# A two-layer decoder trunk on one core: MoBA's queries projected earlier, attention ends behind the softmax, compressed values a step later, x transposed in fewer goes

## The chip, the core and the metric

The kernel runs on one core of a Trainium2 chip. Five engines run at once, each with its own queue of instructions that it takes in order: TensorE (PE in the profile, its weight loads PEld), VectorE (DVE), ScalarE (ACT), GpSimd (POOL) and SyncE (SP), which issues most DMAs. They wait for each other by semaphores. The metric is the time of one execution on the device, in microseconds (us); lower is better.

## The reference

Two layers, 256 positions, width 1024, all in float32. Each layer is

```
x += 1/2 * SwiGLU(RMSNorm(x))                    # FFN 1: 1024 -> 2816 -> 1024
z  = RMSNorm(x) @ W_in                           # one projection, 4888 columns, split:
                                                 # q_a g kc vc ks vs kw vw | q_b k_b v_b | gate_a gate_b
A  = NSA(...)                                    # 8 heads: compressed + selected + sliding window, per-head gates
B  = MoBA(q_b, k_b, v_b)                         # 8 heads; with 256 positions one causal block
x += W_out(sigmoid(gate_a) * (A @ P_A) + sigmoid(gate_b) * (B @ P_B))
x += 1/2 * SwiGLU(RMSNorm(x))                    # FFN 2
```

and a last RMSNorm. The compressed branch takes windows of 32 keys or values at a stride of 16, sends each through a small MLP (2048 -> 128 -> 64, with a GELU between) and attends to the 15 results. Queries and keys of both attentions are turned by rotary positions (rope).

## The kernel before, in words

**Matrices.** Rows are tiled by 128 (two tiles, t = 0 and 1), weights arrive in float32 units of 1 MB and are split into a high and a low part: ScalarE makes `hi` (`split_hi`), VectorE subtracts to make `lo` (`split_lo`). Each product is three matmuls of 512 columns (`mm3`: high x high, low x high, high x low), and each `mm3` is one *tick* of a clock that the program counts while it is written out. Every third tick one half unit of a later weight is split, so `hi` and `lo` instructions stand all through ScalarE's and VectorE's queues.

**The order** of the instructions is written out by hand, with two devices. `defer(n, f)` writes `f`'s instructions n ticks later. A side generator, `attention`, is advanced a step every few ticks between the projections' matmuls (`side_step`): it does the compression, the transposes of keys and queries, and the attention itself, while `project` keeps TensorE busy. `ORDER` lists the projections (each 16 ticks, tile 0 and then tile 1, and after each tile a callback that reads the bank); the place `None` is `hidden`, the first matrix of the compression's MLP. A step of the generator waits for flags such as "KB" (the keys are projected).

**Banks.** PSUM has four tags of two banks each, used in turn: "a0" and "a1" for the large products, "tr" for transposes, "sc" for scores and the small products of the MLP. A tag's next tile waits until everything that reads its last but one tile is done.

**Names.** `kcd`, `ksd`: compressed and selected/window keys; `X2`: the flattened windows; `pK`: transposes of keys, from which ScalarE and VectorE make the high and low `ksT`; `pQ`: transposes of queries, copied to `qT` on ScalarE; `hh`: product of the MLP's first matrix, copied to `HH`; `hp`: two small transposing products of it; `hx`, `hy`, `hth`: the GELU; `hk`, `hv`: its results for keys and values; `cp`: product with the MLP's second matrix (once for keys, once for values); `kc`, `kp`, `kbd`: the compressed keys, roped, transposed, split; `vbd`: the compressed values, spread over the heads. The GELU chain runs in `compress_more`, with `yield` between its steps.

**The callbacks.** `cb_rope` (for q_a, q_b and k_b) makes, per tile, three products and a sum on VectorE (`rt`), for queries a copy to the high part on ScalarE and a subtraction to the low part on VectorE; the gates' callback is one tanh on ScalarE (`gt`).

**The attention loop.** `attend_all` takes the jobs in pairs. In iteration i it writes the values' products of pair i-2 (`s3`: matmuls `o`, and after a group's last job the end `finish`, which on VectorE divides by the sums and applies the gates, `cf` and `aS`), then the transposes of pair i-1 (`s2_`: `pt`) and the scores of pair i (`s1`: `s`), and then the softmax of pair i (`soft`: on VectorE a mask and a maximum for each job, `s` and `m`; on ScalarE the exponentials `P`).

**x transposed.** After the last product of an FFN or of `w_out`, `residual` adds it to x for tile t and column half h and defers four transposes of that quarter of x (`nrm.trans`: one "tr" bank, a product with the gains `xg` on VectorE, a high part on ScalarE and a low part on VectorE, both `hT`).

Of the kernel before, what the change touches and what calls it, by code (L numbers as in the profile page):

```python
# [9 lines left out]
F32 = mybir.dt.float32  # L10
# [7 lines left out]
HD, NH, G = 64, 8, 2  # L18
# [12 lines left out]
C_Q, C_G, C_KV2, C_QB, C_KB, C_VB, C_GA = 0, 512, 920, 1304, 1816, 2328, 2840  # L31
WIDTH = {C_G: 408, C_KV2: 384}

ORDER = [C_Q, C_KV2, C_G, C_GA, None, C_GA + 512, C_QB, C_KB, C_VB, C_GA + 1024, C_GA + 1536]

EVERY = 3
SIDE = 3
# [44 lines left out]
def hybrid_kernel(ctx: ExitStack, tc: tile.TileContext, T, out):  # L82
    nc = tc.nc
# [28 lines left out]
    def bank(tag, name, shape):  # L112

        return psum.tile(shape, F32, name=name, tag=tag)
# [104 lines left out]
    parts, ends = [], []  # L219
# [204 lines left out]
    def ffn(l, n, nrm):  # L424
# [80 lines left out]
        for t in range(NT):  # L505
            for h in range(2):
                if nxt.g is None and t == h == 1:

                    for i in range(2):
                        p = bank("tr", "dq", [128, 256])  # L510
                        for f in range(NF - TAIL, NF):
                            some(f, t, h, p, i)
                        finish(nxt, gfin, ys[t], t, h, p, i)
                    continue
                for f in range(NF - TAIL, NF):
                    some(f, t, h)
                if nxt.g is None:
                    finish(nxt, gfin, ys[t], t, h, ps[t][h])
                else:
                    residual(nxt, t, h, ps[t][h], 4 + t)  # L520
        drop(*tiles)
        return nxt

# [17 lines left out]
    def mixer(l, nrm):  # L541
# [72 lines left out]
        def scaled(name, o, coef):  # L614
            a = s2(name, [128, NH, HD])
            nc.vector.tensor_mul(a, o, coef[:, :, None].to_broadcast([128, NH, HD]))
            return a
# [46 lines left out]
        def compress_more():  # L664
            hx, th = [], []
            for j in range(2):
                hp = bank("sc", "hp", [128, G, 16])
                nc.tensor.matmul(hp.rearrange("p g c -> p (g c)"), HH[:, j], K["sel"][:, j], start=True, stop=True)
                hp = hp[:, :, 0:NC_]

                hx.append(sm.tile([128, G, NC_], F32, name="hx", bufs=2))
                nc.scalar.copy(hx[j], hp)
                y = sm.tile([128, G, NC_], F32, name="hy", bufs=1)
                nc.vector.tensor_mul(y, hx[j], hx[j])
                nc.vector.tensor_scalar(y, y, 0.044715, 1.0, op0=OP.mult, op1=OP.add)
                nc.vector.tensor_mul(y, y, hx[j])
                th.append(sm.tile([128, G, NC_], F32, name="hth", bufs=2))
                nc.scalar.activation(th[j], y, AF.Tanh, scale=float(np.sqrt(2 / np.pi)))
                nc.vector.tensor_scalar(th[j], th[j], 0.5, 0.5, op0=OP.mult, op1=OP.add)
                if j == 0:  # L680
                    nc.vector.tensor_mul(hk.rearrange("p (g c) -> p g c", g=G)[:, :, 0:NC_], th[0], hx[0])
                else:
                    for g in range(G):
                        nc.vector.tensor_mul(hv[:, 4 * g:4 * g + 4, 0:NC_],
                                             th[1][:, g, None, :].to_broadcast([128, 4, NC_]),
                                             hx[1][:, g, None, :].to_broadcast([128, 4, NC_]))
                yield None
            cp = bank("sc", "cp", [64, HD])
            nc.tensor.matmul(cp, hk, w2[0], start=True, stop=True)
            t1 = sm.tile([64, HD], F32, name="ct1", bufs=1)  # L690
            nc.vector.tensor_mul(t1, cp, K["ropec"][:, 0:HD])
            t2 = sm.tile([64, HD], F32, name="ct2", bufs=1)
            for a, b in ((0, 32), (32, 0)):
                nc.vector.tensor_mul(t2[:, a:a + 32], cp[:, b:b + 32], K["ropec"][:, HD + a:HD + a + 32])
            kc2 = sm.tile([64, 2, HD], F32, name="kc2", bufs=1)
            nc.vector.tensor_add(kc2, t1[:, None, :].to_broadcast([64, 2, HD]), t2[:, None, :].to_broadcast([64, 2, HD]))
            cp = bank("sc", "cp", [128, HD])
            nc.tensor.matmul(cp, hv.rearrange("p h c -> p (h c)"), w2[1], start=True, stop=True)
            vbd[0] = p2.tile([128, NH, HD], F32, name="vbd", tag="vbd", bufs=1)
            nc.vector.tensor_mul(vbd[0], cp[:, None, :].to_broadcast([128, NH, HD]),  # L700
                                 K["hmask"][:, :, None].to_broadcast([128, NH, HD]))
            yield None
            kp = bank("tr", "kp", [128, G, 32])
            nc.tensor.transpose(kp.rearrange("p g c -> p (g c)"), kc2.rearrange("p u d -> p (u d)"), ident[:64, :64])
            nc.scalar.copy(kbd[:, :, 0], kp[:, :, 0:16])
            nc.vector.tensor_sub(kbd[:, :, 1], kp[:, :, 0:16], kbd[:, :, 0].bitcast(F32))

        HH = sm.tile([128, 2, CMP_HIDDEN], F32, name="HH", bufs=1)

# [15 lines left out]
        def attend_all(jobs, behind):  # L725

            pairs = [jobs[i:i + 2] for i in range(0, len(jobs), 2)] + [[]] * 2
            for i in range(len(pairs)):
                for j in pairs[i - 2]:
                    j[3]()  # L730

                for a in range(2):
                    for k, d in ((2, 1), (0, 0)):
                        for j in pairs[i - d][a:a + 1]:
                            j[k]()
                for j in pairs[i]:
                    j[1]()
                side["every"] = PAIR + 1 if i == 0 else PAIR if i < len(pairs) - 1 else behind
                yield None
            side["every"] = SIDE  # L740

        def compressed(t, qT, dst):
# [28 lines left out]
            def s3():  # L771
                o = bank("a1", "co", [128, NH, HD])
                nc.tensor.matmul(o, st["pT"], vbd[0], start=True, stop=True)
                nc.gpsimd.tensor_add(dst, dst, scaled("aC", o, st["c"]))

            return s1, soft, s2_, s3

        def attend(t, heads, nj, qT, kT, v, finish):
# [6 lines left out]
            for i0 in range(0, len(items), per):  # L785
# [33 lines left out]
                def s3(i0=i0, some=some, st=st):  # L819
                    if i0 == 0:  # L820
                        O["o"] = bank("a1", "o", [128, NH, HD])
                    for i, (h, j) in enumerate(some):
                        for c in range(nk):
                            nc.tensor.matmul(O["o"][:, i0 + i], st["pT"][:, i * nk + c], v(h, c, j),  # L824
                                             start=c == 0, stop=c == nk - 1)
                    if i0 + per == len(items):
                        finish(O["o"], O["su"])

                yield s1, soft, s2_, s3

# [127 lines left out]
        nxt = Norm(3 * l + 2)  # L958
        for h in range(2):
            project((l, "w_out", h), lambda k, t: (mT[t][0][:, k], mT[t][1][:, k]), KD, 512,  # L960
                    lambda t, ps: residual(nxt, t, h, ps, 4 + t if h else 17))
        drop(*sA, *sB, *gts[0], *gts[1])
        return nxt

# [79 lines left out]
```

## Time and profile before

| | |
|---|---|
| median of 3 runs | 1176.99 us (1176.88 to 1177.00) |
| the profiled execution's own time | 1177.28 us |
| its span, first to last instruction | 1175.2 us |
| mean granted TensorE clock over the span | 0.998 of full speed |
| PE busy | 1161.5 us (99%) |
| DVE busy | 730.2 us (62%) |
| ACT busy | 586.9 us (50%) |
| DMA, mean over the span | 173 GB/s, no queue over 53% of the 16 engines |

Busy is the time with an instruction running. TensorE's instructions overlap, and the ends of its matmuls are modelled, so the distance from one start to the next tells more of its pace than the sum of their lengths. The timeline used below lists one engine's instructions in order of time: start, length, the line of the kernel, what is written from what, the shape, how many in a row, and in brackets the idle time ahead of it with what ended it. The two layers run the same program, 578.7 us apart in the mixer.

### The profile page before, as it was taken

How to read it: one execution, taken by the hardware profiler on the slowest of the kernel's cores; microseconds unless marked ns; L12 is line 12 of the kernel's file. 1: busy time of each engine (PE TensorE's matmuls, PEld its weight loads, DVE VectorE, ACT ScalarE, POOL GpSimd, SP SyncE). 2: the span in 40 equal slices, each digit the busy share in tenths (PEclk: the TensorE clock that was granted, in tenths of full speed). 3: DMA queues.
4: the chain of work that ended last, by engine and by line, in shares of the span. 5: the costliest groups of instructions: out<-in, count | busy, mean ns of one | idle time of the engine just before them, and what ended most of it. 6: DMA issues, size and time to landing. Idle time of an engine off the chain costs nothing.

```text
span 1175.2 us, 14436 instructions
## 1 busy us (share of the span) xinstructions
PE 1161.5 (99%) x5689; PEld 974.8 (83%) x5689; DVE 730.2 (62%) x1003; ACT 586.9 (50%) x929; POOL 31.2 (3%) x46
## 2 busy tenths in 40 slices
PE   8999999999999999999999999999999999999997
PEld 6888888988888888888888888889888888888886
DVE  6645546878857665545475455478787577645543
ACT  6444443567465464445364444346665644545332
POOL 2000000000100000000000000000001000000000
PEclk9999999999999999999999999999999999999999
DMA  8755462862444465555546555538434364665540
GB/s 278 258 194 179 144 243 93 208 193 94 143 143 145 143 236 193 185 174 214 180 154 204 187 188 199 174 117 217 144 109 144 117 204 125 238 208 164 180 179 36
DMA packets 103347, 203.53 MB, mean 173 GB/s; under 512 B 4560, under 2 KB 25504, under 8 KB 103280
## 3 DMA queue, kind: packets, MB, share of 16 engines
q1 hardware_dynamic: 102544, 201.84, 52.6%
q8 instruction: 45, 0.74, 0.3%
q10 hardware_dynamic: 432, 0.46, 0.1%
q0 software_dynamic: 304, 0.32, 0.1%
q14 instruction: 22, 0.18, 0.0%
HBM read 201.55 MB, written 1.05 MB: 172 GB/s over the span
## 4 chain that ended last, share of the span: by engine, by line
PE 90%; DVE 5%; ACT 3%; issue 1%; DMA 1%; SPq 0%; POOL 0%; POOLq 0%; DVEq 0%; ACTq 0%
PE pr L147 7%; PE pr L149 7%; PE pr L148 7%; PE dn L149 7%; PE dn L147 7%; PE dn L148 7%; PE u L147 6%; PE u L148 6%; PE u L149 6%; PE g L148 6%; PE g L147 6%; PE g L149 6%; PE pT L383 2%; DVE lo L237 2%; PE o L824 2%; PE gu L147 1%
## 5 line engine op out<-in xcount | busy, mean ns | idle before, releaser
L237 DVE TENSOR_TENSOR lo<-raw,hi 128x1024 fp32r<-128x1024 f32 (+3 forms) x386 | 457.0, 1214 | 209.0 <-ACT hi L230 208.7
L230 ACT CAST hi<-raw 128x1024 fp32r<-128x1024 f32 (+3 forms) x386 | 386.0, 1040 | 269.2 <-PE u L149 106.7
L147 PE MATMUL pr<-hi,hT 128*128 128x512 f32 (+2 forms) x320 | 126.0, 394 | 0.0
L147 PE MATMUL dn<-hi,aTh 128*128 128x512 f32 x318 | 124.6, 392 | 0.0
L147 PE MATMUL u<-hi,hT 128*128 128x512 f32 x320 | 124.6, 389 | 0.0
L149 PE MATMUL u<-hi,hT 128*128 128x512 f32 x320 | 124.5, 389 | 0.0
L148 PE MATMUL u<-lo,hT 128*128 128x512 f32 x320 | 124.5, 389 | 0.0
L149 PE MATMUL dn<-hi,aTl 128*128 128x512 f32 x318 | 123.8, 389 | 0.0
L148 PE MATMUL dn<-lo,aTh 128*128 128x512 f32 x318 | 123.7, 389 | 0.0
L147 PE MATMUL g<-hi,hT 128*128 128x512 f32 x312 | 123.6, 396 | 0.0
L148 PE MATMUL g<-lo,hT 128*128 128x512 f32 x312 | 121.7, 390 | 0.6 <-DVE lo L237 0.5
L149 PE MATMUL pr<-hi,hT 128*128 128x512 f32 (+2 forms) x320 | 122.0, 381 | 0.0
L148 PE MATMUL pr<-lo,hT 128*128 128x512 f32 (+2 forms) x320 | 121.7, 380 | 0.0
L149 PE MATMUL g<-hi,hT 128*128 128x512 f32 x312 | 121.7, 390 | 0.0
L385 DVE TENSOR_TENSOR aTl<-pT,aTh 128x512 fp32r<-128x512 f32 x40 | 25.8, 686 | 72.5 <-ACT aTh L384 72.5
L149 PEld LDWEIGHTS u<-hi,hT 128*128 128x128 f32 x320 | 60.1, 188 | 12.5
L147 PEld LDWEIGHTS u<-hi,hT 128*128 128x128 f32 x320 | 60.1, 188 | 12.5
L148 PEld LDWEIGHTS u<-lo,hT 128*128 128x128 f32 x320 | 60.1, 188 | 12.4
L149 PEld LDWEIGHTS dn<-hi,aTl 128*128 128x128 f32 x318 | 59.7, 188 | 12.4
L148 PEld LDWEIGHTS dn<-lo,aTh 128*128 128x128 f32 x318 | 59.7, 188 | 12.2
L147 PEld LDWEIGHTS dn<-hi,aTh 128*128 128x128 f32 x318 | 59.7, 188 | 12.0
L148 PEld LDWEIGHTS g<-lo,hT 128*128 128x128 f32 x312 | 58.7, 188 | 12.7 <-DVE lo L237 1.4
(221 smaller groups left out, 1584.8 us busy)
## 6 DMA issues: line engine op xcount, KB each, us to landing
raw<-in_ffn_wd SPq DMA_DIRECT2D x44, 1024.0 KB, 5.0
raw<-in_ffn_wu SPq DMA_DIRECT2D x40, 1024.0 KB, 5.1
raw<-in_ffn_wg SPq DMA_DIRECT2D x38, 1024.0 KB, 5.1
raw<-in_w_in SPq DMA_DIRECT2D x32, 1024.0 KB, 5.1
raw<-in_w_out SPq DMA_DIRECT2D x8, 1024.0 KB, 5.0
raw<-in_ffn_wg SPq DMA_DIRECT2D x10, 512.0 KB, 4.0
raw<-in_ffn_wu SPq DMA_DIRECT2D x8, 512.0 KB, 5.0
raw<-in_w_branch_nsa SPq DMA_DIRECT2D x4, 1024.0 KB, 5.1
```

The source lines that it names most:

```text
L147: nc.tensor.matmul(ps, x[0], w[0], start=start, stop=False)
L148: nc.tensor.matmul(ps, x[0], w[1], start=False, stop=False)
L149: nc.tensor.matmul(ps, x[1], w[0], start=False, stop=stop)
L230: nc.scalar.copy(done[i][0][:, a], raws[i][:, a])
L237: nc.vector.tensor_sub(lo[:, a], raws[i][:, a], hi[:, a].bitcast(F32))
L383: nc.tensor.transpose(p[:, k], src[:, 128 * k:128 * k + 128], ident)
L385: defer(1, lambda: nc.vector.tensor_sub(lo, p, hi.bitcast(F32)))
L824: nc.tensor.matmul(O["o"][:, i0 + i], st["pT"][:, i * nk + c], v(h, c, j), start=c == 0, stop=c == nk - 1)
```

## The change

Four edits. In `ORDER`, the projection of MoBA's queries (`C_QB`) moves to the place ahead of `None`, where the first half of the first gate (`C_GA`) stood; that half moves behind `None`, and the second half into the place that the queries left. In `attend_all`, the end of a group of heads is written after the softmax of the iteration rather than ahead of it. In `compress_more`, the values' `cp` and `vbd` move a step later, behind the keys' transpose `kp`. In `residual`'s waits, the second half of tile 0 is transposed in the tick of the first half of tile 1 (FFN), and the first half of tile 0 in the tick of its second (`w_out`). No arithmetic changes.

```diff
-ORDER = [C_Q, C_KV2, C_G, C_GA, None, C_GA + 512, C_QB, C_KB, C_VB, C_GA + 1024, C_GA + 1536]
+ORDER = [C_Q, C_KV2, C_G, C_QB, None, C_GA, C_GA + 512, C_KB, C_VB, C_GA + 1024, C_GA + 1536]
...
-                    residual(nxt, t, h, ps[t][h], 4 + t)
+                    residual(nxt, t, h, ps[t][h], 8 if h > t else 4 + t * h)
...
             nc.vector.tensor_add(kc2, t1[:, None, :].to_broadcast([64, 2, HD]), t2[:, None, :].to_broadcast([64, 2, HD]))
+            yield None
+            kp = bank("tr", "kp", [128, G, 32])
+            nc.tensor.transpose(kp.rearrange("p g c -> p (g c)"), kc2.rearrange("p u d -> p (u d)"), ident[:64, :64])
+            nc.scalar.copy(kbd[:, :, 0], kp[:, :, 0:16])
+            nc.vector.tensor_sub(kbd[:, :, 1], kp[:, :, 0:16], kbd[:, :, 0].bitcast(F32))
             cp = bank("sc", "cp", [128, HD])
             nc.tensor.matmul(cp, hv.rearrange("p h c -> p (h c)"), w2[1], start=True, stop=True)
             vbd[0] = p2.tile([128, NH, HD], F32, name="vbd", tag="vbd", bufs=1)
             nc.vector.tensor_mul(vbd[0], cp[:, None, :].to_broadcast([128, NH, HD]),
                                  K["hmask"][:, :, None].to_broadcast([128, NH, HD]))
-            yield None
-            kp = bank("tr", "kp", [128, G, 32])
-            nc.tensor.transpose(kp.rearrange("p g c -> p (g c)"), kc2.rearrange("p u d -> p (u d)"), ident[:64, :64])
-            nc.scalar.copy(kbd[:, :, 0], kp[:, :, 0:16])
-            nc.vector.tensor_sub(kbd[:, :, 1], kp[:, :, 0:16], kbd[:, :, 0].bitcast(F32))
...
-                for j in pairs[i - 2]:
-                    j[3]()
+                ends = [j[3]() for j in pairs[i - 2]]
...
                 for j in pairs[i]:
                     j[1]()
+                for end in ends:
+                    if end is not None:
+                        end()
...
-                nc.gpsimd.tensor_add(dst, dst, scaled("aC", o, st["c"]))
+                return lambda: nc.gpsimd.tensor_add(dst, dst, scaled("aC", o, st["c"]))
...
-                    if i0 + per == len(items):
-                        finish(O["o"], O["su"])
+                    return (lambda: finish(O["o"], O["su"])) if i0 + per == len(items) else None
...
-                    lambda t, ps: residual(nxt, t, h, ps, 4 + t if h else 17))
+                    lambda t, ps: residual(nxt, t, h, ps, 4 + t if h else 20 - 3 * t))
```

How instructions stand in the queues, at three places of layer 0.

ScalarE, from the projection ahead of `hidden` (its callbacks are `gt` or `qb`) to the copy of `hh`; before:

```order
L230 CAST hi<-raw 128x1024
L920 ACTIVATE gt<-pr,rh 128x512
L230 CAST hi<-raw 128x1024
L601 CAST ksT<-pK_1876 128x512
L601 CAST ksT<-pK_1882 128x512
L588 CAST qT<-pQ 128x512 x2
L920 ACTIVATE gt<-pr,rh 128x512
L230 CAST hi<-raw 128x1024
L588 CAST qT<-pQ 128x512 x2
L230 CAST hi<-raw 128x1024 x2
L721 COPY HH<-hh 128x256
```

And now:

```order
L230 CAST hi<-raw 128x1024
L535 CAST qb<-rt_1864 128x8x64
L230 CAST hi<-raw 128x1024
L601 CAST ksT<-pK_1883 128x512
L601 CAST ksT<-pK_1889 128x512
L588 CAST qT<-pQ 128x512 x2
L535 CAST qb<-rt_1931 128x8x64
L230 CAST hi<-raw 128x1024
L588 CAST qT<-pQ 128x512 x2
L230 CAST hi<-raw 128x1024 x2
L721 COPY HH<-hh 128x256
```

The two tanh, which read TensorE's bank, have become two copies, which read VectorE's sums `rt`; all else stands where it stood.

VectorE in the same stretch; before:

```order
L658 TENSOR_TENSOR X_1501<-x_1839,X_1501 128x8x2x15
L237 TENSOR_TENSOR lo<-raw,hi 128x1024 x2
L602 TENSOR_TENSOR ksT<-pK_1876,ksT 128x512
L602 TENSOR_TENSOR ksT<-pK_1882,ksT 128x512
L237 TENSOR_TENSOR lo<-raw,hi 128x1024 x5
L674 TENSOR_TENSOR hy<-hx 128x30
```

And now (the rope of tile 0, and the first row of that of tile 1):

```order
L237 TENSOR_TENSOR lo<-raw,hi 128x1024
L528 SCALAR_TENSOR_TENSOR rt_1864<-pr,r,ropeq 128x512
L532 SCALAR_TENSOR_TENSOR rt_1866<-pr,r,ropeq 128x8x32 x2
L534 TENSOR_TENSOR rt_1864<-rt_1864,rt_1866 128x512
L536 TENSOR_TENSOR qb<-rt_1864,qb 128x8x64
L237 TENSOR_TENSOR lo<-raw,hi 128x1024
L602 TENSOR_TENSOR ksT<-pK_1883,ksT 128x512
L602 TENSOR_TENSOR ksT<-pK_1889,ksT 128x512
L237 TENSOR_TENSOR lo<-raw,hi 128x1024
L528 SCALAR_TENSOR_TENSOR rt_1931<-pr,r,ropeq 128x512
```

One rope with its two waiting ends stands ahead of the `ksT` subtractions, the other behind them and one `lo`; both have left the attention loop.

VectorE from the compressed keys to the first scores; before:

```order
L691 TENSOR_TENSOR ct_2042<-cp,c_ropec 64x64
L694 TENSOR_TENSOR ct_2044<-cp,c_ropec 64x32 x2
L696 TENSOR_TENSOR kc_2047<-ct_2042,ct_2044 64x128
L700 TENSOR_TENSOR vbd<-cp,c_hmask 128x512
L237 TENSOR_TENSOR lo<-raw,hi 128x1024
L706 TENSOR_TENSOR kbd<-kp,kbd 128x2x16
L802 TENSOR_TENSOR s<-s,c_causal 128x512
```

And now:

```order
L691 TENSOR_TENSOR ct_2058<-cp,c_ropec 64x64
L694 TENSOR_TENSOR ct_2060<-cp,c_ropec 64x32 x2
L696 TENSOR_TENSOR kc_2063<-ct_2058,ct_2060 64x128
L237 TENSOR_TENSOR lo<-raw,hi 128x1024
L701 TENSOR_TENSOR kbd<-kp,kbd 128x2x16
L705 TENSOR_TENSOR vbd<-cp,c_hmask 128x512
L804 TENSOR_TENSOR s<-s,c_causal 128x512
```

`vbd` has gone behind one `lo` and `kbd`. On TensorE the values' `cp` stands between `kp` and the eight `s`, where it stood right behind the keys' `cp`.

## Rows read from the trace of the kernel before

**Rows 1.** Page: TensorE's busy time, share of the span, instructions.
```profile
PE 1161.5 (99%) x5689; PEld 974.8 (83%) x5689; DVE 730.2 (62%) x1003; ACT 586.9 (50%) x929; POOL 31.2 (3%) x46
```

**Rows 2.** TensorE's waits in all: total us, times, longest us.
```profile
PE pt L815 <- ACT P L807: 1.3, 2, 0.7
PE cp L698 <- issue: 1.2, 2, 0.6
```

**Rows 3.** Timeline of TensorE, compressed keys to attention: start, length, what.
```profile
250.60 0.33 PE L689 MATMUL cp<-w,hk 128*64 128x64 f32 x2
251.55 0.41 PE L698 MATMUL cp<-w,hv 128*128 128x64 f32 x2 [0.62 <-issue]
...
254.01 0.27 PE L704 MATMUL kp<-c_ident,kc 64*128 64x64 f32 x1
254.21 1.22 PE L796 MATMUL s<-ksT,qT 128*128 128x256 f32 x8
255.27 0.40 PE L147 MATMUL pr<-hi,hT 128*128 128x512 f32 x1
```

**Rows 4.** Timeline of VectorE in the same stretch.
```profile
252.94 0.28 DVE L696 TENSOR_TENSOR kc<-ct,ct 64x128 f32<-64x128 f32 x1
253.15 0.68 DVE L700 TENSOR_TENSOR vbd<-cp,c_hmask 128x512 f32<-128x512 f32 x1
253.75 1.21 DVE L237 TENSOR_TENSOR lo<-raw,hi 128x1024 fp32r<-128x1024 f32 x1
254.89 0.18 DVE L706 TENSOR_TENSOR kbd<-kp,kbd 128x32 fp32r<-128x32 f32 x1
254.99 0.70 DVE L802 TENSOR_TENSOR s<-s,c_causal 128x512 f32<-128x512 f32 x1
```

**Rows 5.** Timeline of TensorE, two steps of the attention loop.
```profile
271.56 1.89 PE L824 MATMUL o<-vv,pT 128*128 128x64 f32 x16
...
275.09 0.39 PE L147 MATMUL pr<-hi,hT 128*128 128x512 f32 x1
...
278.52 1.89 PE L824 MATMUL o<-vv,pT 128*128 128x64 f32 x16
...
283.35 0.39 PE L147 MATMUL pr<-hi,hT 128*128 128x512 f32 x1
```

**Rows 6.** Timeline of VectorE between those steps: rope of MoBA's queries, tile 0.
```profile
273.21 0.74 DVE L528 SCALAR_TENSOR_TENSOR rt<-pr,r,ropeq 128x512 f32<-128x512 f32 x1
...
276.16 0.69 DVE L536 TENSOR_TENSOR qb<-rt,qb 128x512 fp32r<-128x512 f32 x1 [0.69 <-ACT qb L535]
```

**Rows 7.** Timeline of ScalarE around `hidden`.
```profile
234.86 0.68 ACT L920 ACTIVATE gt<-pr,rh 128x512 f32<-128x512 f32 x1
...
236.38 1.08 ACT L601 CAST ksT<-pK 128x512 fp32r<-128x512 f32 x2
...
241.59 1.07 ACT L230 CAST hi<-raw 128x1024 fp32r<-128x1024 f32 x1
...
245.38 0.42 ACT L721 COPY HH<-hh 128x256 f32<-128x256 f32 x1
```

**Rows 8.** Timeline of VectorE around `hidden`.
```profile
234.39 2.35 DVE L237 TENSOR_TENSOR lo<-raw,hi 128x1024 fp32r<-128x1024 f32 x2
237.00 1.29 DVE L602 TENSOR_TENSOR ksT<-pK,ksT 128x512 fp32r<-128x512 f32 x2 [0.25 <-ACT ksT L601]
...
242.69 1.22 DVE L237 TENSOR_TENSOR lo<-raw,hi 128x1024 fp32r<-128x1024 f32 x1 [3.27 <-ACT hi L230]
```

**Rows 9.** Timeline of TensorE around `hidden`.
```profile
239.41 1.03 PE L587 MATMUL pQ<-c_ident,qa 128*128 128x128 f32 x8
...
245.85 0.41 PE L668 MATMUL hp<-c_sel,HH 128*128 128x32 f32 x2
```

**Rows 10.** Timeline of TensorE, one go of x's transposes, end of an FFN.
```profile
190.63 0.60 PE L347 MATMUL pT<-c_ident,x 128*128 128x128 f32 x4
```

**Rows 11.** Stretch, us, busy us of PE, PEld, DVE, ACT, POOL; PEclk; DMA share, GB/s.
```profile
1167.50:1175.20 7.70, 0.03 (x1) 0.00 (x0) 2.70 (x11) 1.63 (x5) 0.66 (x1) 0.67 0.28 105
```

## The prediction

> **What bounds the kernel now.** I read the page's list of engines first [rows 1]: TensorE shows 99% busy, so the change can only gain what TensorE loses in waits, and it loses as soon as something else is late. The list of who waited for whom names, after the start-up, only two such waits of TensorE, once in each layer [rows 2]: the compressed values' `cp` matmul and the attention's transposes `pt`, which wait for ScalarE's exponentials. Then I read four stretches of layer 0 in the timeline, engine by engine; layer 1 repeats them, so each term below counts twice. All "new" times are estimates on the clock of the trace of before, put together by hand from its rows in the new order of the queues.
>
> **Part 1: the values a step later.** Now `cp` for the values stands right behind `cp` for the keys and sits idle 0.62 us; it starts 0.95 us after its neighbour (251.55 against 250.60) [rows 3]. In the new order `cp` for the values stands between `kp` and the eight score matmuls `s` that open the attention, so that wait goes and TensorE reaches `kp` 0.95 us sooner, at about 253.06. But `kp` needs `kc`, which VectorE ends at 252.94 + 0.28 = 253.22 [rows 4]: about 0.2 of the gain is lost there. What is late next is worse. The tag "sc" has two banks. The second four of the eight `s` take the bank that `cp` for the values has just filled, and they must wait until VectorE has made `vbd` from it. In the old order `vbd` was done long before. In the new one VectorE does `kc`, one `lo` (1.14 us from its start to the next instruction's), the small `kbd`, and only then `vbd`: 253.15 + 1.14 + 0.10 + 0.68 = 255.1 [rows 4]. Four `s` take half of 255.27 - 254.21 = 1.06 us [rows 3], so the projection goes on at 255.1 + 0.53 = 255.6; now it does at 255.27. The part costs 0.35 us a layer. The ends: a gain of 0.95 if nothing waits, a loss of about 1.4 if ScalarE's `kbd` copy also comes behind a whole `hi` (1.07 [rows 7]). I take 0.35, since each step of it has a row.
>
> **Part 2: ends behind the softmax, and no rope inside the attention.** An undisturbed step runs from the first `o` at 271.56 to the next projection at 275.09, 3.53 us; the disturbed one from 278.52 to 283.35, 4.83 us [rows 5]. It lost 1.30 us. In between VectorE did the rope of MoBA's queries and its wait for ScalarE's copy (273.21 to 276.16, then 0.69) [rows 6], one `lo`, and the end of a group of heads, all ahead of the softmax. Both the rope and the end leave this place, some 4 us of VectorE's queue, so 1.30 a layer comes back. GA's second half takes the slot, and its callback is one tanh on ScalarE, 0.68 [rows 7], in place of a copy of about that length: nothing. The list of waits would price the loss at only 0.7 [rows 2]; the spacing of starts gives 1.30, since records of a delayed matmul are drawn longer too. The Trainium skill, "Trainium Kernel Development and Optimization", section Performance Expectations, says that matmul busy time is a bad metric because matmuls are pipelined; read by busy and idle alone, the term would be 0.65 and the forecast 1.3 us higher; the spacing here agrees with the Trainium skill. I take 1.30 and keep 0.65 as the other end. The same edit at `B` moves an end where TensorE has no wait in the list: nothing.
>
> **Part 3: MoBA's queries ahead of the compression's MLP.** This decides the sign. The first half of GA gave VectorE nothing to do; QB gives it two ropes. In the old order VectorE ran two `lo` from 234.39 (2.35 us), the two `ksT` subtractions at 237.00, one `lo`, and then sat idle 3.27 us until 242.69 [rows 8]. ScalarE did the tanh at 234.86 and the `ksT` copies at 236.38 [rows 7]. TensorE's transposes `pQ` at 239.41 use the two "tr" banks that the `ksT` subtractions have emptied [rows 9]. One rope takes 276.16 - 0.69 - 273.21 = 2.26 us until its sum is ready, ScalarE's copy holds VectorE another 0.69, and the subtraction takes 0.69 [rows 6].
> New order, step by step. VectorE: first `lo` to 235.5; rope of tile 0 until 237.8; copy; subtraction 238.5 to 239.2; `lo` to 240.3; `ksT` subtractions (1.29) to 241.6. ScalarE, which takes its instructions in order, stands at the copy of `qb` until 237.8, and only then does a `hi` and the `ksT` copies (to about 240.4, in time). So `pQ`, due at 239.41, gets its first bank at about 240.95 and its second at 241.55; by the old pace the second four start 0.5 after the first, at 239.9. TensorE is 1.7 us late.
> It goes on. VectorE does another `lo` (to 242.7) and the rope of tile 1 (to 244.9). ScalarE waits for that one too: its second copy runs at 244.9, and the `hi` that stood at 241.59 starts at about 245.4, 3.8 us later. From that `hi` to the end of `HH` ScalarE has no idle time now (241.59 to 245.38 + 0.42, 4.21 us) [rows 7], so `HH` is ready at 249.6 instead of 245.8, and `hp`, which started on it at 245.85 [rows 9], starts at about 249.65. TensorE is 3.8 us late there: 1.7 at `pQ` and 2.1 more at `hp`, both with the whole projection queued behind. Everything that follows (`hy`, `hk`, `kc`) hangs on `hp` and shifts by the same, so nothing is given back. The ends: at least 1.7, if `HH` had slack; at most 2 x (2.26 + 0.69 + 0.69) = 7.3 us, if all the time added to VectorE lands on TensorE. Taking the idle 3.27 off the 7.3 leaves 4.0, close to 3.8. I take 3.8.
>
> **Part 4: x transposed in fewer goes.** Three FFN ends and two output projections merge two goes of four transposes into one of eight. A go of four shows 0.60 us [rows 10], one of eight 1.03 [rows 9], so at most 0.17 a merge, 0.85 in all, and less because the next matmul starts inside the record. The other side: the first half's high and low parts are now made some four triples of matmuls before they are read, about 2.8 us (three triples lie between 251.55 and 254.01 [rows 3]), and VectorE has two products, one residual and one difference of the size of `vbd` (0.68 [rows 4]) to do, 2.7 us, of which the transposes' own time hides part. That fits closely; at worst 0.5 is lost at each of five places. I take 0.
>
> **Sum.** Per layer 0.35 - 1.30 + 3.8 = +2.85 us, twice +5.7. The profiled execution took 1177.28 us, so 1183.0; it lies 0.29 above the median of the runs, 1176.99, so the forecast is **1182.7 us**. With the smaller ends (queries 2.8, values 0, softmax -1.30) it is +3.0, 1180.0; with the larger ones (4.0, 1.0, -0.65) +8.7, 1185.7.
>
> **The rivals.**
> Not slower: the ropes fit VectorE's idle 3.27 us and `pQ` and `HH` don't wait, as if the order in the queues were loose. It decides at `pQ`: the `ksT` subtractions would have to be done by 239.41. Then part 3 is nothing, part 1 a gain of 0.95, and the sum is -2 x 2.25 = -4.5: 1172.5. For it: VectorE has that idle time [rows 8]. Against: it lies behind the `ksT` subtractions, and the ropes are queued ahead of them. 7%.
> Half of it: `pQ` waits 1.7, but `HH` isn't late beyond that, because ScalarE catches up. Per layer 1.7 + 0.35 - 1.30 = 0.75, total +1.5: 1178.5, no change that counts. It decides whether ScalarE finds 2.1 us between 245.4 and `HH`; the rows show it without a gap there [rows 7]. 11%.
> The clock falls: both new waits stand close together, and TensorE's granted clock could drop from 2.4 to 1.2 GHz. After the last matmul the mean granted clock is 0.67 over 7.70 us [rows 11], so some 5.1 us of it stood at half. If each layer had such a stretch with work in it, it would lose 2.5 us more, 1187.7. Against: the waits are about 1.5 and 2 us with matmuls between, and no stretch inside the kernel shows a lower clock now. 10%. The Trainium skill, "TensorE: Matmul & The Clock Gate", Part 1, says the slow clock is the default and steady work releases it, so idle time gives it back; by that rule this rival happens if the waits are long enough for it, and no run here shows it so far.
>
> **How the numbers follow.** Forecast 72%, half of it 11%, clock 10%, not slower 7%. About 0.2% (2.35 us) is what a measurement of this kernel can tell from no change: faster 8%, same 11%, slower 81%. The range reaches over the half case and the forecast's own range and a little beyond, 1178.0 to 1186.5; it leaves out the clock case and the gain.
>
> **What would show it.** In the changed profile: TensorE's list of waits has `pQ` on VectorE's `ksT` (about 1.5 us each) and `hp` on ScalarE's `HH` (about 2 us each); ScalarE's copies of `qb` show idle time of 2 us and more before them; `pt` on `P` and the wait of the values' `cp` are gone; `s` waits for VectorE's `vbd` (about 0.8 us). It would be wrong if `pQ` starts within 0.5 us of its old place, or if `HH` follows `hh` at once.

## The result

| | before | after |
|---|---|---|
| median of 5 runs | 1177.00 us (1176.88 to 1177.46) | 1186.53 us (1184.98 to 1187.30) |
| the profiled execution's own time | 1177.28 us | 1187.30 us |
| its span | 1175.2 us | 1185.2 us |
| mean granted clock over the span | 0.998 | 0.995 |

The ratio is 1.0074, with a 95% interval of 1.0062 to 1.0085: the change makes the kernel 9.5 us slower. The forecast was 1182.7 with a range of 1178.0 to 1186.5; the sign and the largest mechanism came as forecast, but the loss is 3.8 us larger and the median lies at the very end of the range (0.03 us beyond it). In five of the fourteen profiles, that of the changed kernel among them, the granted clock also drops once within the first 16 us (to a mean of 0.57 to 0.67 between 8 and 12 us), which puts TensorE 1.2 to 1.9 us behind the trace of before. Probably for that reason the times of one kernel gather in two groups (the kernel before at 1177.1 and at 1178.5), so parts below 1.5 us are read from the traces as well as from the medians.

The page after answers to [rows 1]: TensorE's busy time grew by 4 us though it runs the same 5689 matmuls.

```profile
PE 1165.5 (98%) x5689; PEld 976.7 (82%) x5689; DVE 731.9 (62%) x1003; ACT 587.7 (50%) x929; POOL 36.7 (3%) x46
```

TensorE's waits after, against the two of [rows 2] (total us, times, longest us); the start-up's are left out:

```profile
PE pQ L587 <- DVE ksT L602: 3.0, 2, 1.5
PE hp L668 <- ACT HH L721: 2.3, 2, 1.1
...
PE pr L148 <- DVE lo L237: 1.2, 2, 0.6
PE pr L147 <- DVE rt L532: 1.2, 2, 0.6
PE s L798 <- DVE vbd L705: 0.9, 2, 0.7
```

`pt` and `cp` are gone. In their place stand five waits, each once in each layer. Three were named ahead (`pQ`, `hp`, `s`), two were not: `pr` of line 148 for a `lo`, and `pr` of line 147 for a rope's `rt`. Where they stand and what they cost shows best from start to start. TensorE around `hidden` after, to be read against [rows 9]:

```profile
241.49 0.39 PE L149 MATMUL pr<-hi,hT 128*128 128x512 f32 x1
243.38 1.25 PE L587 MATMUL pQ<-c_ident,qa 128*128 128x128 f32 x8 [1.50 <-DVE ksT L602]
...
249.15 0.39 PE L147 MATMUL pr<-hi,hT 128*128 128x512 f32 x1
250.14 0.50 PE L148 MATMUL pr<-lo,hT 128*128 128x512 f32 x1 [0.60 <-DVE lo L237]
250.48 0.40 PE L149 MATMUL pr<-hi,hT 128*128 128x512 f32 x1
252.01 0.41 PE L668 MATMUL hp<-c_sel,HH 128*128 128x32 f32 x2 [1.14 <-ACT HH L721]
```

Undisturbed, one of these matmuls starts 0.23 us behind the other. `pQ` starts 1.89 behind its neighbour (1.66 lost), the `pr` 0.99 (0.76 lost), `hp` 1.53 (1.30 lost): 3.72 us a layer, all behind the two ropes. Set against the trace of before, the loss is 3.9: the same matmul lies 2.3 us behind just ahead of `pQ` (239.18 before, 241.49 after) and 6.2 behind at the keys' `cp` (250.60 and 256.77). Before, `hp` already started 0.40 behind its neighbour, so 1.1 of its 1.30 is new; and the next matmul behind `pQ` starts 1.01 us after it in place of 0.80.

ScalarE in the same stretch, against [rows 7] (start, length, what, idle time ahead of it and its releaser):

```profile
240.24 0.62 ACT L535 CAST qb<-rt 128x512 fp32r<-128x512 f32 x1 [2.97 <-DVE rt L534]
...
241.71 1.07 ACT L601 CAST ksT<-pK 128x512 fp32r<-128x512 f32 x2
...
247.26 0.62 ACT L535 CAST qb<-rt 128x512 fp32r<-128x512 f32 x1 [2.00 <-DVE rt L534]
247.78 1.04 ACT L230 CAST hi<-raw 128x1024 fp32r<-128x1024 f32 x1
248.73 1.06 ACT L588 CAST qT<-pQ 128x512 fp32r<-128x512 f32 x2
249.69 2.00 ACT L230 CAST hi<-raw 128x1024 fp32r<-128x1024 f32 x2
251.58 0.38 ACT L721 COPY HH<-hh 128x256 f32<-128x256 f32 x1
```

ScalarE stands 2.97 and 2.00 us at the two copies of `qb`, with `ksT`, `hi` and `HH` queued behind them. From the second copy to `HH` it has no gap: that is the path to `hp`. VectorE's rows of the same stretch show the other half:

```profile
237.94 0.75 DVE L528 SCALAR_TENSOR_TENSOR rt<-pr,r,ropeq 128x512 f32<-128x512 f32 x1
...
240.89 0.69 DVE L536 TENSOR_TENSOR qb<-rt,qb 128x512 fp32r<-128x512 f32 x1 [0.69 <-ACT qb L535]
241.50 1.22 DVE L237 TENSOR_TENSOR lo<-raw,hi 128x1024 fp32r<-128x1024 f32 x1
242.64 1.28 DVE L602 TENSOR_TENSOR ksT<-pK,ksT 128x512 fp32r<-128x512 f32 x2
...
248.86 1.23 DVE L237 TENSOR_TENSOR lo<-raw,hi 128x1024 fp32r<-128x1024 f32 x1 [0.26 <-ACT hi L230]
```

The subtractions of `ksT`, on which `pQ` waits, come behind the rope, the stand for ScalarE's copy, the rope's subtraction and a `lo`; the idle 3.27 of [rows 8] is gone. The last row is the `lo` that the `pr` of line 148 waits for; it waits itself for a `hi` behind ScalarE's second copy.

The disturbed step of [rows 5] is whole again:

```profile
278.14 1.89 PE L826 MATMUL o<-vv,pT 128*128 128x64 f32 x16
...
281.66 0.39 PE L147 MATMUL pr<-hi,hT 128*128 128x512 f32 x1
```

3.52 us in place of 4.83.

**The wait that nobody forecast** stands earlier, where the first FFN's end runs into the mixer's projections. TensorE, first matmul of the projection `C_G` (408 columns):

```profile
218.45 0.34 PE L149 MATMUL pr<-hi,hT 128*128 128x384 f32 x1
219.38 0.43 PE L147 MATMUL pr<-hi,hT 128*128 128x408 f32 x1 [0.59 <-DVE rt L532]
```

It starts 0.93 behind its neighbour, 0.75 more than the usual 0.18. It needs the bank of tag "a0" that `C_KV2`'s tile 0 holds until VectorE's rope has read it. VectorE at the FFN's end, after:

```profile
201.58 0.15 DVE L357 TENSOR_SCALAR v<-ss 128x1 f32<-128x1 f32 x1
...
202.65 0.22 DVE L367 SCALAR_TENSOR_TENSOR w<-r,v 128x1 f32<-128x1 f32 x1 [0.66 <-POOL r L361]
...
203.37 0.96 DVE L237 TENSOR_TENSOR lo<-raw,hi 128x768 fp32r<-128x768 f32 x1
```

and before:

```profile
198.15 0.15 DVE L372 TENSOR_SCALAR rh<-r 128x1 f32<-128x1 f32 x1
...
200.92 0.96 DVE L237 TENSOR_TENSOR lo<-raw,hi 128x768 fp32r<-128x768 f32 x1
```

Before, tile 0's root (`v`, `w`, `r`, `rh`) was done by 198.3, ahead of the last residual. With the second half of x transposed together with the other tile's first half, the sum of squares comes later. The root and a second pair of products (`xg`, `hT`) now stand ahead of the first `lo` of `C_KV2`, with VectorE idle 0.66 us for POOL's `r`; which of the two weighs more was not told apart. Everything that VectorE does after it, the ropes of the queries and of `C_KV2` included, is that much later against TensorE.

**The clock.** The second mixer of the same execution has one stretch at a lower granted clock. Stretch, us, busy us of PE, PEld, DVE, ACT, POOL, then PEclk, DMA share and GB/s:

```profile
831.00:835.00 4.00, 2.27 (x14) 1.51 (x13) 3.05 (x4) 4.00 (x7) 0.00 (x0) 1.00 0.21 81
835.00:839.00 4.00, 4.00 (x13) 3.17 (x13) 2.67 (x7) 1.83 (x5) 0.00 (x0) 0.57 0.84 287
```

The first stretch holds the waits of `pr` and `hp`, with TensorE busy 2.27 of 4.00 us. In the second the mean is 0.57, so most of it stood at 1.2 in place of 2.4 GHz. Against 1.00 that takes away up to (1 - 0.57) x 4 = 1.7 us. Before, the same place showed 1.00. The one run whose mean clock was 0.998 took 1184.98 us, the other four, at 0.995 to 0.996, 1186.10 to 1187.30. That difference isn't the mixer's alone: this execution has the drop in the start-up too (0.64 between 8 and 12 us), which puts TensorE 1.4 us behind, and a mean clock doesn't tell the two apart.

### The profile page after: what moved, and what is told of

Its sections match the earlier page's. It is cut to its first block, busy times and chain, and to the rows that moved or that the text cites. A ratio compares the mean times of both kernels' runs of the same rounds, so it can differ in the third digit from the quotient of the medians.

```text
span 1185.2 us, 14426 instructions
## 1 busy us (share of the span) xinstructions
PE 1165.5 (98%) x5689; PEld 976.7 (82%) x5689; DVE 731.9 (62%) x1003; ACT 587.7 (50%) x929; POOL 36.7 (3%) x46
## 4 chain that ended last, share of the span: by engine, by line
PE 89%; DVE 6%; ACT 2%; issue 1%; DMA 0%; POOL 0%; SPq 0%; POOLq 0%; DVEq 0%; ACTq 0%
PE dn L149 7%; PE dn L147 7%; PE pr L147 7%; PE dn L148 7%; PE pr L149 6%; PE pr L148 6%; PE u L147 6%; PE u L148 6%; PE u L149 6%; PE g L148 6%; PE g L149 6%; PE g L147 6%; PE o L826 3%; PE pT L383 2%; DVE lo L237 2%; PE s L798 2%
## 5 line engine op out<-in xcount | busy, mean ns | idle before, releaser
L147 PEld LDWEIGHTS pr<-hi,hT 128*128 128x128 f32 x320 | 60.5, 189 | 11.3 <-ACT hi L230 1.7
```

The source lines that it names most:

```text
L147: nc.tensor.matmul(ps, x[0], w[0], start=start, stop=False)
```

## The experiments

Each kernel was timed beside the kernel before on the same chip (its median in the three groups of runs: 1177.42, 1177.27 and 1178.44).

**1. The queries alone.** Only the order of the projections of the change.

```diff
-ORDER = [C_Q, C_KV2, C_G, C_GA, None, C_GA + 512, C_QB, C_KB, C_VB, C_GA + 1024, C_GA + 1536]
+ORDER = [C_Q, C_KV2, C_G, C_QB, None, C_GA, C_GA + 512, C_KB, C_VB, C_GA + 1024, C_GA + 1536]
```

> The kernel before with the new order of projections alone (MoBA's queries ahead of the MLP, GA's first half behind it). Theory: the loss sits here, 3.9 us a layer of TensorE waiting at pQ (about 1.5) and at hp (about 2.3, drawn as 1.1 in the list), less what the rope's leaving the attention gives back by itself, between 0 and 1.3 a layer: 1182.2 to 1184.8 us, and up to 2.5 more if the granted clock falls behind those waits. Rival, the loss is made by the other three parts: 1177 to 1178 and no pQ or HH wait in the list.

Measured: 1183.41 us (1183.07 to 1184.64), ratio 1.0052 [1.0038, 1.0066], against 1177.42: +6.0. Its waits of TensorE:

```profile
PE pQ L587 <- DVE ksT L602: 3.0, 2, 1.5
...
PE hp L668 <- ACT HH L721: 2.3, 2, 1.1
...
PE pr L148 <- DVE lo L237: 1.2, 2, 0.6
```

The three waits around `hidden` are there in the sizes that the changed kernel has, with the wait for `lo` among them: all three belong to the queries. `pt` is gone too, though the ends stand in their old place: the rope's leaving alone gives the 1.30 a layer back, and 2 x (3.72 - 1.30) = 4.8 of the 6.0 are read from the rows. Same matmul against same matmul, TensorE's lag behind the trace of before grows by 5.15 us from 16 us to the end (1.91 to 7.06). The rest is no larger than what a drop of the clock in the start-up costs; this run's profile has one (0.62 between 8 and 12 us) and none behind it.

**2. The rest without the queries.** The changed kernel with the old `ORDER` (the diff of experiment 1 turned round).

> The changed kernel with the old order of projections: values a step later, ends behind the softmax and x in fewer goes are left. Theory: x costs 0.9 a layer at the end of the first FFN, the values 0.45 a layer, the ends give 0 to 1.3 a layer: 1177.1 to 1179.7 us, no pQ and no HH wait, vbd and the root's wait still there, granted clock as in the kernel before. Rival, these parts carry half of the loss or more: above 1181.5. Second rival, x and values cost nothing and the ends give 1.3: 1174.4.

Measured: 1177.43 us (1176.86 to 1180.09), ratio 1.0005 [0.9996, 1.0014]: no change. So the other three parts together neither cost nor gain. Its waits show that this nothing is a sum:

```profile
PE s L798 <- DVE vbd L705: 1.3, 2, 0.7
PE pr L147 <- DVE rt L532: 1.1, 2, 0.6
```

The two new ones are paid for by `cp` and `pt`, which are gone.

**3. The values alone.** Only the move of `kp` and `kbd` ahead of the values' `cp` and `vbd`.

> The kernel before with the compressed values a step later alone. Theory: the wait of the values' cp (0.6 of idle time, 0.95 from start to start) goes, the second four s wait 0.7 to 0.8 for vbd in the other bank of sc: +0.35 to +0.45 a layer, 1177.7 to 1177.9 us. Rival, the new wait is in the shadow of another: -0.95 a layer, 1175.1 us, and no wait of s for vbd in the list.

Measured: 1177.38 us (1176.88 to 1180.26), ratio 1.0001 [0.9993, 1.0010]: nothing, between the two expectations. The waits:

```profile
PE s L796 <- DVE vbd L705: 1.3, 2, 0.7
PE pt L815 <- ACT P L807: 0.4, 2, 0.2
```

The trade of `cp`'s wait for that of `s` came as forecast, a small loss. It is paid back by something that wasn't: `pt`'s wait falls from 0.7 to 0.2, presumably because the attention comes a little later against the projections.

**4. x at the FFN ends alone.**

```diff
-                    residual(nxt, t, h, ps[t][h], 4 + t)
+                    residual(nxt, t, h, ps[t][h], 8 if h > t else 4 + t * h)
```

> The kernel before with x transposed in fewer goes at the ends of the FFNs alone (the two output projections as before). Theory, from the trace of the changed kernel: at the end of the FFN ahead of the mixer VectorE falls about 1 us further behind, and the first matmul of the projection G waits 0.6 to 0.8 for the rope of KV2: +0.9 a layer, 1178.8 us. Rival, what the prediction had: nothing, 1176.9 to 1177.1 us, and the wait of that matmul in the changed kernel came from another part.

Measured: 1179.26 us (1178.91 to 1180.85), ratio 1.0016 [1.0007, 1.0025]: +1.84, 0.92 a layer. The wait that it makes (those of `pt` and `cp` stay):

```profile
PE pr L147 <- DVE rt L532: 1.1, 2, 0.6
```

This edit alone makes the wait of `C_G`'s first matmul, and it costs what the spacing in the changed kernel (0.75) and the median (0.92) both say.

**5. The ends alone.** Only the hunks of `attend_all`, `compressed` and `attend`: the ends are returned and called behind the softmax.

> The kernel before with the ends of the attention's groups behind the softmax alone (MoBA's queries stay in the attention). Theory: the end of a group of heads is one of the two things ahead of the late softmax, and moving it alone takes the wait of pt for P (0.7 of idle time, 1.1 to 1.3 from start to start) away or most of it: 0.8 to 1.3 a layer, 1174.8 to 1175.8 us. Rival, the rope of MoBA's queries alone makes the softmax late: pt still waits 0.7 for P, 1177.2 to 1177.5 us.

Measured: 1175.19 us (1174.49 to 1176.58), ratio 0.9980 [0.9972, 0.9989], against 1177.27: 2.1 us faster, 1.04 a layer. The step that [rows 5] shows disturbed, in this kernel:

```profile
278.96 1.89 PE L826 MATMUL o<-vv,pT 128*128 128x64 f32 x16
...
282.49 0.39 PE L147 MATMUL pr<-hi,hT 128*128 128x512 f32 x1
```

3.53 us, with MoBA's rope still in the attention. Experiments 1 and 5 together: the rope and the end were both ahead of the softmax, and taking either away is enough. The gain is had once, and the ends give it without moving a projection.

**6. The same work, the copy later.** The changed kernel; ScalarE's copy of the queries' rope is issued four triples behind the rope and VectorE's subtraction one triple behind the copy, for `C_QB` only (`late=4` there, 0 for `C_Q`; the lines that pass `late` on are left out here).

```diff
...
-            nc.scalar.copy(dst[:, :, 0], t1)
-            defer(1, lambda: nc.vector.tensor_sub(dst[:, :, 1], t1, dst[:, :, 0].bitcast(F32)))
+            copy = lambda: nc.scalar.copy(dst[:, :, 0], t1)
+            defer(late, copy) if late else copy()
+            defer(late + 1, lambda: nc.vector.tensor_sub(dst[:, :, 1], t1, dst[:, :, 0].bitcast(F32)))
```

> The changed kernel with one thing moved: ScalarE's copy of the rope of MoBA's queries is issued four triples later, and VectorE's subtraction one triple behind it; the same work on every engine. Theory, the order of the in-order queues makes the loss: the ksT copies no longer stand behind a copy that waits for VectorE, and the ksT subtractions come 2.4 us sooner, so pQ doesn't wait (1.5 before) and HH is up to 2.3 us earlier; 2.6 to 3.9 a layer comes back, 1178 to 1181 us. Rival, the amount of VectorE's new work (2 x 2.95 us against 3.27 idle) makes it: what pQ gains turns up at the next lo or at hp, above 1183.5 us.

Measured: 1179.62 us (1178.89 to 1181.52; one more execution took 6718 us and isn't counted), ratio to before 1.0021 [1.0012, 1.0029]: 6.9 us below the changed kernel, with not one instruction more or less. Its waits of TensorE, where `pQ` no longer appears:

```profile
PE hp L669 <- ACT HH L722: 1.4, 2, 0.7
PE s L799 <- DVE vbd L706: 1.3, 2, 0.7
...
PE pr L147 <- DVE rt L532: 1.1, 2, 0.6
```

VectorE and ScalarE around `hidden`, to be read against their rows after the change. VectorE:

```profile
238.42 0.69 DVE L534 TENSOR_TENSOR rt<-rt,rt 128x512 f32<-128x512 f32 x1
239.03 1.22 DVE L237 TENSOR_TENSOR lo<-raw,hi 128x1024 fp32r<-128x1024 f32 x1
240.16 1.28 DVE L603 TENSOR_TENSOR ksT<-pK,ksT 128x512 fp32r<-128x512 f32 x2
241.36 0.68 DVE L537 TENSOR_TENSOR qb<-rt,qb 128x512 fp32r<-128x512 f32 x1
```

ScalarE:

```profile
237.02 1.06 ACT L602 CAST ksT<-pK 128x512 fp32r<-128x512 f32 x2
239.14 0.62 ACT L535 CAST qb<-rt 128x512 fp32r<-128x512 f32 x1 [1.06 <-DVE rt L534]
```

The `ksT` copies come ahead of the `qb` copy, the `ksT` subtractions one `lo` behind the rope's sum and ahead of its subtraction, and VectorE nowhere stands for ScalarE. From just ahead of `pQ` to the keys' `cp` TensorE now loses 1.2 us against the trace of before (239.18 to 240.38, 250.60 to 253.03) in place of 3.9: the order of the two in-order queues made most of the loss. Over two layers that is some 5.3 of the 6.9; the clock doesn't fall here either. The 1.2 that is left (`pQ` starts 0.52 behind its neighbour, `hp` waits 0.7) is what this order doesn't take away; how much of it the mere amount of VectorE's new work makes was not told apart.

**7. Values with a step of their own.** The kernel before with the values a step later, and a `yield None` behind `vbd`, so that three triples lie between `vbd` and the first `s`; the diff is against the kernel of experiment 3.

```diff
             nc.vector.tensor_mul(vbd[0], cp[:, None, :].to_broadcast([128, NH, HD]),
                                  K["hmask"][:, :, None].to_broadcast([128, NH, HD]))
+            yield None
```

> The kernel before with the compressed values a step later, and one more step of three triples between vbd and the first attention scores. Theory: the wait of the values' cp goes and the new one of s for vbd doesn't come, 0.75 to 0.95 a layer, and the wait of pt for P, which the values alone cut from 0.7 to 0.2, stays at 0 to 0.7: 1174.9 to 1175.9 us. Rival, the later start of the attention makes another wait of the same size (pt for P, or the next projection behind it): 1177.0 to 1177.8 us.

Measured: 1176.60 us (1174.88 to 1177.38), ratio 0.9987 [0.9979, 0.9996]: 0.7 faster by the median, between the two expectations. The profiled execution, 1174.88 us and at a mean clock of 0.999, is as fast as the theory had it; most of the others ran at 0.996 or 0.997, and where the clock falls in those no profile shows. The waits of `cp`, `s` and `pt` are all gone; a new one stands much later, where the compressed branch's values product `co` needs a bank that the last group's end `aS` still reads:

```profile
PE co L774 <- DVE aS L616: 1.1, 2, 0.7
```

**8. Values with a step, ends, and x at the output projections** (old `ORDER`, old FFN ends).

> The kernel before with values a step later and a step of three triples behind vbd, ends behind the softmax, and x in fewer goes at the output projections only; old order of projections, FFN ends as before. Theory, the gains of the parts add up: cp 0.75 to 0.95 and pt 0.8 to 1.3 a layer, the output projections nothing: 1172.7 to 1174.1 us, and no wait of TensorE behind the start-up longer than 0.3. Rival, they overlap, since the later attention already shortens pt's wait: 1174.5 to 1176 us.

Measured: 1175.39 us (1174.45 to 1177.03), ratio 0.9980 [0.9971, 0.9990]. No better than the ends alone: the gains overlap as the rival had it, though for another reason. VectorE ahead of the new wait:

```profile
303.70 0.74 DVE L528 SCALAR_TENSOR_TENSOR rt<-pr,r,c_rope 128x512 f32<-128x512 f32 x1
...
305.26 1.23 DVE L538 TENSOR_TENSOR kb<-rt,rt 128x1024 f32<-128x1024 f32 x1
...
307.11 0.69 DVE L616 TENSOR_TENSOR aS<-o,cf 128x512 f32<-128x512 f32 x1
```

Three triples' delay put the rope of MoBA's keys ahead of the end of the last group, 2.8 us of VectorE's queue.

**9. The changed kernel with the FFN ends as before** (the diff of experiment 4 turned round).

> The changed kernel with the FFN ends as before (x in fewer goes at the output projections only). Theory: only the wait of G's first matmul for the rope of KV2 goes, 0.9 a layer; the wait of a projection's matmul for lo (0.6 a layer) stays, since it stood in the run with the queries alone too: 1183.0 to 1183.5 us where the granted clock doesn't fall, pQ 1.5 and hp 1.1 in the list as before. Rival, VectorE's lag from the FFN end feeds pQ and hp too, so more comes back: 1180 to 1182 us and a pQ wait below 1.2.

Measured: 1184.44 us (1184.11 to 1186.21), ratio 1.0060 [1.0047, 1.0072]. `pQ` waits 1.5 and `hp` 1.1 as in the changed kernel, and the wait for `rt` is gone; beside the changed kernel in the same group of runs (next) it is 2.3 us faster by the medians, 1.2 by the lowest. So the lag of the FFN end doesn't feed the waits around `hidden`; the rival falls. The median is above the forecast, which was for executions without a fall of the clock. The profiled one, 1185.57 us, has one in its start-up (0.67 between 8 and 12 us) and one behind `hp`, here in the first mixer:

```profile
252.00:256.00 4.00, 4.00 (x13) 3.17 (x13) 2.54 (x9) 1.49 (x5) 0.00 (x0) 0.61 0.95 323
```

**10. The changed kernel once more.**

> The changed kernel once more, beside the one above on the same chip: where does TensorE's granted clock fall. Theory: the fall at 835 us of the first profile stands behind the waits of pQ, lo and hp in the second mixer and comes in some executions only; executions without any fall take 1185.0, with one 1.2 to 1.5 more. Rival, falls belong to the start-up alone: no profile shows one behind 20 us again, and the spread of the runs is that of the kernel before (about 2 us).

Measured: 1186.72 us (1185.33 to 1187.68), ratio 1.0073 [1.0061, 1.0086]; the run with a mean clock of 0.998 took 1185.33, those at 0.995 to 0.996 1185.86 to 1187.68. Its profile has the lower clock again, and again right behind `hp` in the second mixer:

```profile
834.00:838.00 4.00, 4.00 (x14) 3.18 (x12) 2.60 (x10) 1.42 (x4) 0.00 (x0) 0.58 0.96 337
```

This execution, 1185.86 us, has no drop in the start-up. So three of the four profiles of kernels with the waits of `pQ`, `pr` and `hp` show a lower clock behind them, in one of the two mixers each, and the fourth (experiment 1) none; of the kernels without that set of waits (the kernel before and experiments 2 to 8, 11 and 12) no profile does between the start-up and the last 20 us. That these waits bring the fall about is likely by this and not shown.

**11 and 12. One triple in place of three, with and without x at the output projections.** Experiment 8 with

```diff
+            side["every"] = 1
             yield None
```

behind `vbd`; experiment 12 has the output projections as before besides.

> The kernel before with values a step later and a step of one triple (in place of three) behind vbd, ends behind the softmax, x in fewer goes at the output projections. Theory: with one triple the end of the last group comes ahead of the rope of KB in VectorE's queue, so the second co doesn't wait (0.5 to 0.7 with three triples), and s still finds vbd done: cp 0.75 to 0.95 and pt 1.1 a layer come back, 1173.2 to 1174.0 us. Rival, one triple is too short and s waits for vbd again, up to 0.7 a layer: 1174.4 to 1175.4 us.

> The kernel above without x in fewer goes at the output projections. Theory: a merge of two goes there is worth nothing that can be measured, at most 0.17 a projection: within 0.4 us of the kernel above. Rival, the first FFN behind the projection waits for the late root as G does behind the FFN: the kernel above is 1 us or more slower than this one.

Measured: 1173.73 us (1173.39 to 1175.25), ratio 0.9967 [0.9954, 0.9979], and 1174.39 us (1173.80 to 1175.55), ratio 0.9971 [0.9960, 0.9982]. Experiment 11's list of TensorE's waits names only the three of the start-up (`pz` and twice `g`): neither `cp` nor `s`, `pt` or `co` waits. This is the best version: some 3.3 us faster than the kernel before (1177.0; 4.7 against the 1178.44 of its own group of runs) and 12.8 faster than the changed one. The output projections' merges, alone between the two, are worth 0.7 by the medians, 0.4 by the lowest and 0.2 by TensorE's lag from 16 us to the end; the intervals overlap, so a small gain is likely and not shown.

## Why the prediction was right, and where it was short

**The queries, +3.8 forecast.** Right, in cause and in size: 3.72 by the spacings, 3.9 against the trace of before, and the cause was put to the test by experiment 6, where the same work in another order takes most of it away. That ScalarE would be held at the `qb` copy is seen twice (2.97 and 2.00 us). One step was off inside: of the 2.1 forecast at `hp` only 1.1 is lost there. ScalarE's second stand also holds up the `hi` behind it, VectorE's next `lo` starts late for that (at 248.86, after 0.26 idle for the `hi`), and TensorE loses 0.76 on that `lo` first; with the 0.2 behind `pQ`, the three are 2.1. The Trainium skill, "PSUM — Partial Sum Buffer", section Engine vs sequencer instructions, says that the queues of ScalarE and VectorE are strictly first in, first out; the rows of `qb` and `ksT` agree.

**The softmax, -1.30.** The size was right by the spacing (4.83 to 3.52), and the other end, 0.65 by idle time, was wrong. What was short is to whom it was due: the prediction counted on both the rope's leaving and the end's, and experiments 1 and 5 show that either does it alone.

**The values, +0.35.** The mechanism was right (`cp`'s wait gone, `s` late by 0.67 idle for `vbd`). Alone the edit is worth 0 rather than 0.35, because it also shortens `pt`'s wait, which the prediction had left out; in the changed kernel, where `pt` doesn't wait any more, nothing pays for it.

**x in fewer goes, 0 forecast.** This is the term that failed: 1.84 us in the kernel with that edit alone. The prediction weighed the transposes on TensorE and the high and low parts that must be ready for the next product, and gave 0.5 at worst at each of five places; only one place a layer, the FFN's end ahead of the mixer, shows a loss, and it is 0.9. The prediction didn't follow the other thing that hangs on the same step, the sum of squares and the root of tile 0, which VectorE has to take in its queue with a stand for POOL, nor whose bank comes free behind it two projections later.

**The clock.** The rival had 10%, and it came true in part: in the profiles one mixer, not both, stands at the lower clock behind `hp`, for up to 1.7 us, and the net loss is about 1.0 where the rival had 2.5 a layer. The argument against it, that the waits are too small and have matmuls between, was an argument from nothing measured. The Trainium skill, "TensorE: Matmul & The Clock Gate", Part 1, says that the throttled state is the default and activity releases it, and that the same kernel shows a varying number of slow matmuls at its start from run to run. The three profiles agree in so far as each fall stands behind a stretch with TensorE busy 2.27 of 4.00 us, and as it varies from run to run: the first mixer once, the second twice, and in the other five mixers of these four profiles the same stretch, busy 2.27 to 2.28, is followed by no fall.

**The sum.** In both profiles of the changed kernel the lag of the same matmul behind the trace of before grows by 3.8 us in layer 0 (16.28 and 591.19 before, 17.69 and 596.42 in the first profile, 16.31 and 594.97 in that of experiment 10): 0.9 ahead of `pQ`, 3.9 from there to the keys' `cp`, 0.4 at the values, and -1.3 at the late softmax. In layer 1, where the clock falls, it grows by 4.8. The low clock takes 1.5 there, and 0.5 of it comes back at once, since `s` then waits 0.2 in place of 0.7 for `vbd`. Two layers without a fall make 7.6; the run at a mean clock of 0.998 stands 8.0 above before (1184.98 against 1177.00), so 0.4 is open. Against the forecast's +5.7 the 9.5 has 1.8 more from x and 0.1 from the other parts; the last 1.9 is the 0.4 that is open and falls of the clock, of which those in the start-up, 1.4 us in the profiled execution, aren't the change's.

## What to carry to other kernels

An engine that takes its instructions in order pays for a wait with everything queued behind it: before an operation is moved, write out for both of two engines that hand work to each other what stands behind the hand-over, and issue the second half only when the first will be done. A wait with two causes gives its gain once, so try the cheaper cause alone. And when a step is delayed to merge it with another, follow all that hangs on it (here a root with a hop over POOL), through to the bank that it frees.

## What the hardware showed that was not expected

Waits of 0.6 and 1.1 us within 2 us of each other, behind one of 1.5 some 7 us earlier, were followed in three of four profiles, in one of the two mixers each, by 4 us at a mean granted clock of 0.57 to 0.61, though TensorE stood still for less than half of the 4 us ahead (busy 2.27 of 4.00). Without the first and the `lo` wait, and with `hp`'s at 0.7 (experiment 6), the clock stayed at 1.00 and the mean at 0.999. In the other five mixers of these four profiles the same waits, with TensorE busy 2.27 to 2.28 of 4.00 us, were followed by no fall, so the waits alone don't decide; what does was not told apart.

A merge of two goes of transposes, worth at most 0.17 us on TensorE, cost 0.9 us a layer on the way over VectorE, POOL and a bank; a step of three triples in place of one cost 1.7 us in all (1175.39 against 1173.73), and the wait behind the rope of MoBA's keys in VectorE's queue is gone with it.
